# DeltaNet block on one core: a chunk's keys meet keys and queries in one product, queries meet both directions' states in one; a shorter inverse root; the last expert's down projection earlier

## The chip, the cores and the metric

The kernel runs on one core of one Trainium2 chip. The time is device microseconds of one execution, the median of three: 1802.84 us (1800.17 to 1805.5). Besides, one execution was profiled; it took 1801.21 us.

## The reference, cut to what matters

One encoder block on x of 1024 tokens by 1024 channels, in f32. One input projection of the normalised x feeds two mixers: a chunked gated linear attention (GLA, 4 heads) and a gated DeltaNet (8 heads of 128, each in both directions). After gates, a sum and an output projection comes a mixture of 32 experts, of which each token uses two, then a final RMSNorm. What one direction of a DeltaNet head computes:

```python
q, k = l2_norm(conv(q)), l2_norm(conv(k))
lower = where(strict, (k * beta) @ k.T * decay, 0)
u, w  = solve(I + lower, v * beta), solve(I + lower, k * beta * exp(g))
attn  = where(tri, q @ k.T * decay, 0)
for c in chunks:
    v_new = u[c] - w[c] @ S
    o[c]  = (q[c] * exp(g)) @ S + attn[c] @ v_new
    S     = exp(g_last) * S + k_tail[c].T @ v_new
```

## The kernel before, in words

**Number formats.** Large products (projections, experts) split each f32 operand in a high and a low fp32r part and add three products (`mm3`, L81 to L83); weights come by DMA as `wraw`, ScalarE rounds them to `whi` (L113) and VectorE takes the remainder `wlo` (L115). Small products in the DeltaNet are plain f32, and each shows as two records on TensorE (PE).

**Order.** The tile framework's scheduler puts the instructions of each engine into one order when the program is built, from the order in which the code is written and its own estimate of how long each takes. At run time each engine takes its list in that order and waits by semaphores. So a change of the code can move projection products far from the place that was edited.

**DeltaNet, 8 heads** (about 140 to 960 us of the span). Three stages per head:
- `gdn_stage1`: the projections of k, q and v, each followed by `conv` (ScalarE copies to `cin`, VectorE adds five taps at L302/L304, SiLU by ScalarE and L311) and transposes with sums of squares (L321). The keys of each 128-token chunk meet themselves (L354, tile `pgm`, four chunks of 128x128 in a bank) and the queries (L379, `pqk`). VectorE multiplies these 128x512 banks with the decays `e` into the strictly lower part M (L364) and the attention A (L382). M goes to DRAM (`xs_d`) and comes back as 32x32 blocks. VectorE inverts these in 62 instructions (`V`, L409/L411, "the solve"); the result goes to DRAM (`vs_d`, L415) and back as `Ua` (L425).
- `gdn_stage2`: per direction a transpose of `Ua` (L428), then four small groups of products that put the 32x32 inverses together (L447, L453, L461, L466, "the fix-ups"), each fed by a copy of the one before (L450, L455/L457, L463, L467). Then the scan over 8 chunks, the forward (`cf`) and the backward (`cb`) direction in turn: k·S (L479), r on VectorE (L481), q·S (L483), U·r (L486), a copy `vn` on ScalarE (L488), kt·vn (L492), the new state S on VectorE (L495), A·vn (L500). The outputs add up in `oac` (L503 to L507), and ScalarE squares them (L510).
- `gdn_stage3`: norm and gate of the outputs (inverse root L67 to L76, L529), transposes (L531), L533, and a store to `mixT`.

TensorE fills the waits of these chains with projection products (L81 to L83): those of the next heads, and 16 `gate_task`s (L276 to L280, called by `run_tasks`, two after most heads).

**After the DeltaNet** the GLA prepares its gate weights: small loads `prep` on SyncE's queue (L590, L598, L601), casts on three engines up to `ws` (L612), and its first products (L623).

**Experts.** For each expert `moe_up` (gate and up projections into `pgu`, then `sg` at L1090/L1091), `moe_down` of the expert before (`py`, `y` at L1112, and a scatter with addition by GpSimd, L1113), `moe_turn` (transposes L1097, `hh` L1100). After the last scatter the sums are read back (L1187), normalised with `rsqrt(n=2)` and stored (L1198).

**`rsqrt`** (L61): a shift, a subtraction from a magic number, a halving, then three Newton steps of three instructions.

Of the kernel before, what the change touches and what calls it, by code (L numbers as in the profile page):

```python
# [8 lines left out]
F32 = mybir.dt.float32  # L9
F32R = mybir.dt.float32r  # L10
BF = mybir.dt.bfloat16
# [7 lines left out]
P = 128  # L19
# [16 lines left out]
def hybrid_kernel(ctx: ExitStack, tc: tile.TileContext, ins, out):  # L36
# [23 lines left out]

    def rsqrt(v, n, name):  # L61

        ti = small.tile([P, n], I32, name=f"rsi{name}", bufs=1)
        y = small.tile([P, n], F32, name=f"rsy{name}")
        a = small.tile([P, n], F32, name=f"rsa{name}", bufs=1)
        xh = small.tile([P, n], F32, name=f"rsx{name}", bufs=1)
        ve.tensor_scalar(ti, v.bitcast(I32), 1, None, op0=OP.logical_shift_right)  # L67
        ve.tensor_scalar(y.bitcast(I32), ti, -1.0, RS_MAGIC, op0=OP.mult, op1=OP.add)  # L68
        ve.tensor_scalar(xh, v, -0.5, None, op0=OP.mult)  # L69
        for _ in range(3):  # L70
            if n == 1:
                ve.scalar_tensor_tensor(a, y, y, xh, op0=OP.mult, op1=OP.mult)
            else:
                ve.tensor_mul(a, y, y)  # L74
                ve.tensor_mul(a, a, xh)  # L75
            ve.scalar_tensor_tensor(y, a, 1.5, y, op0=OP.add, op1=OP.mult)  # L76
        return y

    def mm3(o, l, r, start, stop):
# [16 lines left out]
    with mix:  # L96
# [193 lines left out]
            gp.memset(zt[d], 0.0)  # L290

        def gdn_stage1(h, finish=None):
            def conv(nm, c0):
# [7 lines left out]
                a = gd.tile([P, T], F32, name="acc", bufs=5)  # L301
# [26 lines left out]

            ka = conv("k", C_DK)
# [15 lines left out]

            if finish:
                finish()
            A, M = {}, {}  # L350
            for hf in range(2):
                pgm = bank("tp", 2)
                for i in range(4):
                    te.matmul(pgm[:, i], kch[:, 4 * hf + i], kch[:, 4 * hf + i], start=True, stop=True)  # L354
                for d in range(2):
                    e = gd.tile([P, 4, P], F32, name="e", bufs=7)
                    nc.sync.dma_start(e.rearrange("p a b -> p (a b)"),
                                      dap(gcs_d, ((2 * h + d) * NT + 4 * hf) * P, [[0, P], [1, 4 * P]]))
                    with tc.issue_after(k_done):
                        ve.tensor_tensor(e, e, mneg[d][:, None, :].to_broadcast([P, 4, P]), op=OP.add)  # L360
                    for i in range(4):
                        sc.activation(e[:, i], e[:, i], AF.Exp, bias=nb[:, d, 4 * hf + i:4 * hf + i + 1])
                    m = gd.tile([P, 4, P], F32, name="m", bufs=6)
                    ve.scalar_tensor_tensor(m, pgm, -1.0, e, op0=OP.mult, op1=OP.mult)  # L364
                    for b in range(4):
                        nc.sync.dma_start(xs_d[h][d, b, 4 * hf:4 * hf + 4].rearrange("c s t -> s c t"),
                                          m[32 * b:32 * b + 32, :, 32 * b:32 * b + 32])
                    A[d, hf], M[d, hf] = e, m

            qa = conv("q", C_DQ)  # L370
            ss, _ = sumsq("q", qa)
            ve.tensor_scalar(ss, ss, 4 * EPS, None, op0=OP.add)
            rq = rsqrt(ss, NT, "q")
            rqs = small.tile([P, NT], F32, name="rqs")
            ve.tensor_scalar(rqs, rq, float(P ** -0.5), None, op0=OP.mult)
            for hf in range(2):
                pqk = bank("tp", 2)
                for i in range(4):
                    te.matmul(pqk[:, i], kch[:, 4 * hf + i],  # L379
                              qa[:, (4 * hf + i) * P:(4 * hf + i + 1) * P], start=True, stop=True)  # L380
                for d in range(2):
                    ve.tensor_tensor(A[d, hf], pqk, A[d, hf], op=OP.mult)  # L382
            va = conv("v", C_DV)
# [34 lines left out]
        def gdn_stage2(h, st):  # L418
# [52 lines left out]
            S = [None, None]  # L471
            seen = set()
            for step in range(NT):
                for d in range(2):
                    c = step if d == 0 else NT - 1 - step
                    hf, i = divmod(c, 4)
                    pc = bank("cf" if d == 0 else "cb", 1)
                    if step:
                        te.matmul(pc[:, 0], kch[:, c], S[d], start=True, stop=True)  # L479
                        r = gd.tile([P, P], F32, name=f"r{d}", bufs=1)  # L480
                        ve.scalar_tensor_tensor(r, pc[:, 0], NEG[:, d, c, h:h + 1], vtok[:, c],  # L481
                                                op0=OP.mult, op1=OP.add)
                        te.matmul(pc[:, 1], qa[:, c * P:(c + 1) * P], S[d], start=True, stop=True)  # L483
                    else:
                        r = vtok[:, c]
                    te.matmul(pc[:, 2], U[d][:, c], r, start=True, stop=True)  # L486
                    vn = gd.tile([P, P], F32, name=f"vn{d}", bufs=1)
                    sc.copy(vn, pc[:, 2])  # L488
                    if step < NT - 1:
                        kt = gd.tile([P, P], F32, name=f"kt{d}", bufs=2)  # L490
                        sc.activation(kt, ktok[:, c], AF.Copy, scale=ktl[:, d, c:c + 1])
                        te.matmul(pc[:, 0], kt, vn, start=True, stop=True)  # L492
                        Sn = gd.tile([P, P], F32, name=f"S{d}", bufs=2)
                        if step:
                            ve.scalar_tensor_tensor(Sn, S[d], DEC[:, d, c, h:h + 1], pc[:, 0],  # L495
                                                    op0=OP.mult, op1=OP.add)
                        else:
                            ve.tensor_copy(Sn, pc[:, 0])
                        S[d] = Sn
                    te.matmul(pc[:, 3], A[d, hf][:, i], vn, start=True, stop=True)  # L500
                    if step:
                        if c in seen:
                            ve.scalar_tensor_tensor(oac[:, c], pc[:, 1], EG[:, d, c, h:h + 1], oac[:, c],  # L503
                                                    op0=OP.mult, op1=OP.add)
                        else:
                            sc.activation(oac[:, c], pc[:, 1], AF.Copy, scale=EG[:, d, c, h:h + 1])
                        ve.tensor_tensor(oac[:, c], pc[:, 3], oac[:, c], op=OP.add)  # L507
                        if c in seen:
                            jk = gd.tile([P, P], BF, name="jk2", bufs=1)
                            sc.activation(jk, oac[:, c], AF.Square, accum_out=oss[:, c:c + 1])  # L510
                    else:
                        sc.copy(oac[:, c], pc[:, 3])
                    seen.add(c)
            return oac, oss, rq

# [602 lines left out]
    with tc.tile_pool(name="me", bufs=1, reuse_waits="tile") as me:  # L1118
# [22 lines left out]
        for e in range(NE + 1):  # L1141
            if e < NE:
                f = e + NX - 1
                if f < NE:
                    moe_fetch(xbs[f % NX], idx[:, f:f + 1])
                if e + 1 < NE:
                    xs[e + 1] = moe_rows(me, xbs[(e + 1) % NX])
                sg = moe_up(me, w[e], xs.pop(e))
            if e:
                moe_down(me, w.pop(e - 1), hs.pop(e - 1), idx[:, e - 1:e], roww[:, e - 1:e])  # L1150
            if e < NE:
                hs[e] = moe_turn(me, sg)
# [80 lines left out]
```

## Time and profile before

| what | value |
|---|---|
| median of 3 runs | 1802.84 us |
| profiled execution | 1801.21 us, its span 1799.4 us |
| TensorE (PE) busy | 1667.4 us, 93% |
| VectorE (DVE) busy | 1308.0 us, 73% |
| ScalarE (ACT) busy | 946.9 us, 53% |
| mean granted TensorE clock | 0.98 of full speed |

The span is what the trace covers; 1.8 us lie around it. A busy share is the sum of an engine's instructions over the span. TensorE's records overlap their successors, so its share is an upper end of what it needs.

### The profile page before, as it was taken

How to read it: one execution, taken by the hardware profiler on the slowest of the kernel's cores; microseconds unless marked ns; L12 is line 12 of the kernel's file. 1: busy time of each engine (PE TensorE's matmuls, PEld its weight loads, DVE VectorE, ACT ScalarE, POOL GpSimd, SP SyncE). 2: the span in 40 equal slices, each digit the busy share in tenths (PEclk: the TensorE clock that was granted, in tenths of full speed). 3: DMA queues.
4: the chain of work that ended last, by engine and by line, in shares of the span. 5: the costliest groups of instructions: out<-in, count | busy, mean ns of one | idle time of the engine just before them, and what ended most of it. 6: DMA issues, size and time to landing. Idle time of an engine off the chain costs nothing. (4 is left out here: it accounts for less than half of the span.)

```text
span 1799.4 us, 26981 instructions
## 1 busy us (share of the span) xinstructions
PE 1667.4 (93%) x9519; PEld 1364.1 (76%) x9519; DVE 1308.0 (73%) x2904; ACT 946.9 (53%) x2001; POOL 178.0 (10%) x184
## 2 busy tenths in 40 slices
PE   6999999999999999999999999998999799888881
PEld 5778878888888888888887888877778588666670
DVE  6787987777796877867856365565778898777773
ACT  6546464462644536445344353545355688767762
POOL 0000000000000000000001000000000243434410
PEclk9999999999999999999999999999999899999995
DMA  5322222313222232221322122214576699989965
GB/s 151 84 69 64 80 59 84 75 55 94 54 78 70 66 95 58 77 71 36 94 60 64 37 94 64 77 36 148 180 253 250 228 351 331 320 305 328 327 193 198
DMA packets 207681, 241.02 MB, mean 134 GB/s; under 512 B 72679, under 2 KB 154999, under 8 KB 207543
## 3 DMA queue, kind: packets, MB, share of 16 engines
q1 hardware_dynamic: 198327, 222.46, 38.6%
q0 software_dynamic: 9216, 16.81, 4.1%
q8 instruction: 76, 1.25, 0.3%
q14 instruction: 62, 0.51, 0.1%
HBM read 205.44 MB, written 50.53 MB: 142 GB/s over the span
## 5 line engine op out<-in xcount | busy, mean ns | idle before, releaser
L81 PE MATMUL pj<-hT_hi,whi 128*128 128x512 f32 x1168 | 470.8, 403 | 3.8 <-ACT cin L299 2.8
L83 PE MATMUL pj<-hT_hi,wlo 128*128 128x512 f32 x1168 | 470.8, 403 | 0.2 <-DVE wlo L115 0.2
L82 PE MATMUL pj<-hT_lo,whi 128*128 128x512 f32 x1168 | 470.7, 403 | 0.0
L1062 DVE TENSOR_TENSOR elo<-eraw,ehi 128x2048 fp32r<-128x2048 f32 x96 | 219.6, 2290 | 72.4 <-ACT ehi L1061 71.8
L81 PEld LDWEIGHTS pj<-hT_hi,whi 128*128 128x128 f32 x1168 | 220.9, 189 | 43.5 <-ACT cin L299 3.2
L83 PEld LDWEIGHTS pj<-hT_hi,wlo 128*128 128x128 f32 x1168 | 220.7, 189 | 37.7 <-DVE wlo L115 0.9
L82 PEld LDWEIGHTS pj<-hT_lo,whi 128*128 128x128 f32 x1168 | 220.8, 189 | 36.0
L1061 ACT CAST ehi<-eraw 128x2048 fp32r<-128x2048 f32 x96 | 184.1, 1919 | 69.9 <-DMA eraw<-in_moe_w_up_dram 56.9
L113 ACT CAST whi<-wraw 128x512 fp32r<-128x512 f32 x146 | 90.6, 621 | 160.2 <-PE pj L82 158.8
L115 DVE TENSOR_TENSOR wlo<-wraw,whi 128x512 fp32r<-128x512 f32 x146 | 100.3, 687 | 93.9 <-ACT whi L113 82.4
L304 DVE SCALAR_TENSOR_TENSOR acc<-cin,cols,acc 128x1024 f32<-128x1024 f32 x96 | 122.7, 1278 | 1.2
L81 PE MATMUL pgu<-ehi,xh 128*128 128x512 f32 x256 | 105.7, 413 | 0.0
L82 PE MATMUL pgu<-elo,xh 128*128 128x512 f32 x256 | 102.8, 402 | 0.0
L83 PE MATMUL pgu<-ehi,xl 128*128 128x512 f32 x256 | 102.4, 400 | 0.0
L1113 POOL DMA_INDIRECT acc_d<-y,idx x32 | 76.7, 2396 | 199.2 <-ACT xh L1080 74.9
L409 DVE TENSOR_TENSOR prod<-V,X 128x2 f32<-128x2 f32 (+30 forms) x248 | 85.8, 346 | 6.3
L411 DVE TENSOR_REDUCE V<-prod 128x1 f32<-128x2 f32 (+30 forms) x248 | 84.5, 341 | 5.8
L1068 POOL DMA_INDIRECT xb<-h_d,idx x32 | 66.8, 2088 | 149.3 <-ACT xb L1123 132.8
L276 ACT ACTIVATE gth<-pj 128x512 f32<-128x512 f32 x64 | 38.0, 593 | 80.0 <-PE pj L83 80.0
L83 PEld LDWEIGHTS pgu<-ehi,xl 128*128 128x128 f32 x256 | 48.9, 191 | 12.0
L81 PEld LDWEIGHTS pgu<-ehi,xh 128*128 128x128 f32 x256 | 49.3, 193 | 10.7 <-ACT xh L1080 0.2
L82 PEld LDWEIGHTS pgu<-elo,xh 128*128 128x128 f32 x256 | 49.1, 192 | 10.4
(408 smaller groups left out, 3255.1 us busy)
## 6 DMA issues: line engine op xcount, KB each, us to landing
wraw<-in_w_in_dram SPq DMA_DIRECT2D x144, 256.0 KB
eraw<-in_moe_w_gate_dram SPq DMA_DIRECT2D x64, 512.0 KB
eraw<-in_moe_w_up_dram SPq DMA_DIRECT2D x64, 512.0 KB
eraw<-in_moe_w_down_dram SPq DMA_DIRECT2D x32, 1024.0 KB
e<-gcs_d SPq DMA_DIRECT2D x32, 256.0 KB
gate_d<-gateT SPq DMA_DIRECT2D x16, 512.0 KB
xx<-in_x_dram SPq DMA_DIRECT2D x8, 512.0 KB
gin<-gate_d SPq DMA_DIRECT2D x8, 512.0 KB
```

What stands on the lines that cost most here:

```text
L81: te.matmul(o, lh, rh, start=start, stop=False)
L82: te.matmul(o, lh, rl, start=False, stop=False)
L83: te.matmul(o, ll, rh, start=False, stop=stop)
L113: sc.copy(hi, raw)
L115: ve.tensor_tensor(lo, raw, hi.bitcast(F32), op=OP.subtract)
L304: ve.scalar_tensor_tensor(a, cin[:, tp:tp + T], cw(wi, tp), a, op0=OP.mult, op1=OP.add)
L409: ve.tensor_tensor(pr_[:, :mc, :i + 1], V[:, :mc, :i + 1], X[:, i, :i + 1][:, None, :].to_broadcast([P, mc, i + 1]), op=OP.mult)
L411: ve.tensor_reduce(V[:, :mc, i], pr_[:, :mc, :i + 1], axis=AX.X, op=OP.add)
L1061: sc.copy(hi, raw)
L1062: ve.tensor_tensor(lo, raw, hi.bitcast(F32), op=OP.subtract)
L1068: gp.indirect_dma_start(out=xb, out_offset=None, in_=h2_d[:, :], in_offset=bass.IndirectOffsetOnAxis(ap=si, axis=0), bounds_check=T - 1, o ...
L1113: gp.indirect_dma_start(out=acc_d[:, :], out_offset=bass.IndirectOffsetOnAxis(ap=si, axis=0), in_=y, in_offset=None, bounds_check=T - 1, o ...
```

## The change

1. `rsqrt`: shift and subtraction become one instruction that works on the integer read as a number (times -0.5, plus the magic number); for n over 1 the halving goes too. 12 instructions become 10 (9 become 8 for n = 1).
2. `conv` writes into a tile that it is given. k and q of a head lie in one tile `kq`, so that the products k·k and k·q of a chunk are one product with 256 columns (64 instead of 128 products). A PSUM tile `pkq` holds two chunks, so VectorE takes M and A out in pieces of 128x256 instead of 128x512. All products come after q's convolution; loads and exponentials of `e` are issued before it.
3. The states of both directions stay in a tile `SK`. q·S is computed only when the scan comes to a chunk the second time, for both directions in one product of 256 columns (64 products instead of 112). The outputs of a chunk's first visit are then a plain copy.
4. For the last expert `moe_down(30)` is issued ahead of `moe_up(31)`.

```diff
-        ve.tensor_scalar(ti, v.bitcast(I32), 1, None, op0=OP.logical_shift_right)
-        ve.tensor_scalar(y.bitcast(I32), ti, -1.0, RS_MAGIC, op0=OP.mult, op1=OP.add)
-        ve.tensor_scalar(xh, v, -0.5, None, op0=OP.mult)
+        ve.tensor_scalar(y.bitcast(I32), v.bitcast(I32), -0.5, RS_MAGIC, op0=OP.mult, op1=OP.add)
...
-                ve.tensor_mul(a, a, xh)
+                ve.scalar_tensor_tensor(a, a, -0.5, v, op0=OP.mult, op1=OP.mult)
...
+            kq = gd.tile([P, 2, T], F32, name="kq", bufs=2)
+            ka, qa = kq[:, 0], kq[:, 1]
+            conv("k", C_DK, ka)
...
+                for i in (0, 2):
+                    pkq = psum.tile([P, 2, 2, P], F32, name="pkq", tag="tp", bufs=2)
+                    for j in range(2):
+                        c = 4 * hf + i + j
+                        te.matmul(pkq[:, j], kch[:, c], kq[:, :, c * P:(c + 1) * P], start=True, stop=True)
+                    for d in range(2):
+                        e = A[d, hf][:, i:i + 2]
+                        ve.scalar_tensor_tensor(M[d, hf][:, i:i + 2], pkq[:, :, 0], -1.0, e,
+                                                op0=OP.mult, op1=OP.mult)
+                        ve.tensor_tensor(e, pkq[:, :, 1], e, op=OP.mult)
...
-                        te.matmul(pc[:, 1], qa[:, c * P:(c + 1) * P], S[d], start=True, stop=True)
+                        if c in seen:
+                            ds = [o for o in range(2) if c != (0, NT - 1)[o]]
+                            te.matmul(pc[:, 2:2 + len(ds)], qa[:, c * P:(c + 1) * P],
+                                      SK[:, c, ds[0]:ds[-1] + 1], start=True, stop=True)
...
+                if e == NE - 1:
+                    moe_down(me, w.pop(e - 1), hs.pop(e - 1), idx[:, e - 1:e], roww[:, e - 1:e])
                 sg = moe_up(me, w[e], xs.pop(e))
-            if e:
+            if e and e != NE - 1:
```

The scheduler's order changes with it in most of the DeltaNet. In the changed program the line numbers of that part are about 5 higher (L447 is L452, L453 is L458, L461 is L466).

The first place is TensorE at the fix-ups of the first direction (`Ub`, `m` and `zt` are their operands; `pj` are projection products). Before, in a middle head:

```order
L447 MATMUL pz<-Ub_6924,m 32x32 x16
L82 MATMUL pj<-hT_lo,whi 128x512
L83 MATMUL pj<-hT_hi,wlo 128x512
L81 MATMUL pj<-hT_hi,whi 128x512
L82 MATMUL pj<-hT_lo,whi 128x512
L83 MATMUL pj<-hT_hi,wlo 128x512
L81 MATMUL pj<-hT_hi,whi 128x512
L82 MATMUL pj<-hT_lo,whi 128x512
L83 MATMUL pj<-hT_hi,wlo 128x512
L81 MATMUL pj<-hT_hi,whi 128x512
L453 MATMUL pu<-Ua_6918,zt_476 64x64 x8
L82 MATMUL pj<-hT_lo,whi 128x512
```

and in a middle head of the change:

```order
L81 MATMUL pj<-hT_hi,whi 128x512
L82 MATMUL pj<-hT_lo,whi 128x512
L83 MATMUL pj<-hT_hi,wlo 128x512
L452 MATMUL pz<-Ub_4443,m 32x32 x16
L458 MATMUL pu<-Ua_4437,zt_460 64x64 x8
L466 MATMUL pz<-Ub_4443,m 64x64 x8
L81 MATMUL pj<-hT_hi,whi 128x512
```

The nine projection products between the first two groups, and those before the third, now stand ahead of the first group.

The second place is TensorE at the end of the eighth head's scan (`cb` the backward direction, `mg` the transposes of the outputs). Of the change:

```order
L508 MATMUL cf<-vn_9410,e 128x128
L486 MATMUL cb<-SK,kq 128x128
L492 MATMUL cb<-SK,kq 128x128
L496 MATMUL cb<-r_9419,Ub_9142 128x128
L508 MATMUL cb<-vn_9423,e 128x128
L536 MATMUL mg<-ident,oac 128x128 x8
L81 MATMUL pj<-hT_hi,whi 128x512
```

Before, the transposes were these rows, with 27 projection products between the last product of the scan and them:

```order
L83 MATMUL pj<-hT_hi,wlo 128x512
L81 MATMUL pj<-hT_hi,whi 128x512
L82 MATMUL pj<-hT_lo,whi 128x512
L531 MATMUL mg<-ident,oac 128x128 x8
L83 MATMUL pj<-hT_hi,wlo 128x512
```

The whole scan of the eighth head has no projection product in the change, and had one to three between most steps before; behind the transposes stand 41 projection products up to the GLA's first gate product (L628), where there were 80 (up to L623).

The third place is ScalarE at the last two experts (`sg` is up, `hh` the turned hidden rows, `y` down). Before:

```order
L1100 CAST hh<-pht 128x256
L1061 CAST ehi<-eraw 128x2048
L1090 ACTIVATE sg<-pgu 128x256
L1112 ACTIVATE y<-py,roww 128x512 x2
L1100 CAST hh<-pht 128x256
```

and in the change:

```order
L1105 CAST hh<-pht 128x256
L1066 CAST ehi<-eraw 128x2048
L1117 ACTIVATE y<-py,roww 128x512 x2
L1095 ACTIVATE sg<-pgu 128x256
L1105 CAST hh<-pht 128x256
```

The rows `y` of expert 30 come ahead of `sg` of expert 31.

## Rows read from the trace of the kernel before

**Rows 1.** The page: busy time, share and instructions of each engine.
```profile
PE 1667.4 (93%) x9519; PEld 1364.1 (76%) x9519; DVE 1308.0 (73%) x2904; ACT 946.9 (53%) x2001; POOL 178.0 (10%) x184
```
**Rows 2.** Windows: a middle head; length, busy time (instructions) of each engine, clock, DMA.
```profile
480.00:590.00 110.00, 108.97 (x683) 90.46 (x681) 85.86 (x209) 52.26 (x155) 3.33 (x13) 1.00 0.27 71
```
**Rows 3.** Waits of TensorE in the DeltaNet: total us, times, longest.
```profile
PE cb L492 <- ACT vn L488: 4.6, 5, 1.0
```
**Rows 4.** Timeline, ScalarE in a scan: start us, us, what.
```profile
579.68 1.28 ACT L345 ACT_TABLE_LOAD   x1
```
**Rows 5.** Timeline, f32 products of 128 and of 256 columns (first to last record).
```profile
225.63 1.16 PE L354 MATMUL tp<-acc 128*128 128x128 f32 x8
...
1048.74 1.03 PE L740 MATMUL gpo<-gR,gqd 128*128 128x256 f32 x4
```
**Rows 6.** Groups of VectorE by form: count, busy us, mean ns, idle before.
```profile
L304 DVE SCALAR_TENSOR_TENSOR acc<-cin,cols,acc 128x1024 f32<-128x1024 f32 x93 | 118.9, 1278 | 1.0
L364 DVE SCALAR_TENSOR_TENSOR m<-tp,e 128x512 f32<-128x512 f32 x32 | 21.8, 687 | 3.9 <-ACT e L362 3.7 <-PE pz L461 0.2
...
L1091 DVE TENSOR_TENSOR sg<-pgu,sg 128x256 f32<-128x256 f32 x32 | 13.4, 418 | 2.0 <-ACT sg L1090 2.0
```
**Rows 7.** Timeline, VectorE in the last inverse roots.
```profile
1778.03 0.17 DVE L67 TENSOR_SCALAR rsif<-ssf 128x2 int32<-128x2 int32 x1
...
1778.24 0.17 DVE L68 TENSOR_SCALAR rsyf<-rsif 128x2 int32<-128x2 int32 x1
```
**Rows 8.** Timeline, three places of the tail: GpSimd's scatters of experts 29, 30, 31.
```profile
1749.45 1.55 POOL L1113 DMA_INDIRECT acc_d<-y,idx  x1 [7.23 <-ACT hh L1100]
...
1758.02 1.55 POOL L1113 DMA_INDIRECT acc_d<-y,idx  x1 [7.02 <-ACT hh L1100]
...
1765.12 1.55 POOL L1113 DMA_INDIRECT acc_d<-y,idx  x1 [5.55 <-issue]
```
**Rows 9.** Timeline, fix-ups of the eighth head, two projection products ahead of them.
```profile
903.04 0.39 PE L83 MATMUL pj<-hT_hi,wlo 128*128 128x512 f32 x1
903.27 0.39 PE L81 MATMUL pj<-hT_hi,whi 128*128 128x512 f32 x1
903.59 1.20 PE L447 MATMUL pz<-Ub,m 128*32 128x32 f32 x32
...
906.07 1.15 PE L453 MATMUL pu<-Ua,zt 128*64 128x64 f32 x16
...
908.04 1.14 PE L461 MATMUL pz<-Ub,m 64*64 64x64 f32 x16
```
**Rows 10.** Timeline, one hand-over in a scan.
```profile
946.13 0.39 PE L486 MATMUL cb<-r,Ub 128*128 128x128 f32 x2
...
946.87 0.49 PE L492 MATMUL cb<-vn,kt 128*128 128x128 f32 x2
```
**Rows 11.** Timeline, the eighth head's solve on VectorE and the transpose behind its DMAs.
```profile
863.36 0.15 DVE L409 TENSOR_TENSOR prod<-V,X 128x2 f32<-128x2 f32 x1
...
890.45 0.68 DVE L411 TENSOR_REDUCE V<-prod 128x16 f32<-128x512 f32 x1
...
901.79 1.24 DVE L428 STREAM_TRANSPOSE Ub<-Ua 128x1024 f32<-128x1024 f32 x1
```
**Rows 12.** Timeline, from the scan's last product to the GLA's first gate product.
```profile
951.82 0.49 PE L500 MATMUL cb<-vn,e 128*128 128x128 f32 x2
...
958.71 1.23 PE L531 MATMUL mg<-ident,oac 128*128 128x128 f32 x8 [0.24 <-DVE oac L529]
...
969.48 0.35 SPq L280 DMA_DIRECT2D gate_d<-gateT  x1
...
978.66 0.59 PE L623 MATMUL pz<-ws,gs 98*128 98x256 f32 x3 [0.55 <-DVE ws L612]
```
**Rows 13.** In the GLA: a wait of TensorE, and windows from its end (columns as rows 2).
```profile
1247.93 1.08 PE L679 MATMUL tp<-ident,gki 128*128 128x128 f32 x4 [4.09 <-DVE gki L675]
...
1248.00:1252.00 4.00, 4.00 (x22) 4.00 (x23) 2.71 (x8) 2.22 (x5) 0.00 (x0) 0.59 0.82 267
```

More of the change, by code (lines that the diff above doesn't have):

```diff
@@ L61, in rsqrt @@
     def rsqrt(v, n, name):
-        ti = small.tile([P, n], I32, name=f"rsi{name}", bufs=1)
         y = small.tile([P, n], F32, name=f"rsy{name}")
         a = small.tile([P, n], F32, name=f"rsa{name}", bufs=1)
-        xh = small.tile([P, n], F32, name=f"rsx{name}", bufs=1)
-        ve.tensor_scalar(ti, v.bitcast(I32), 1, None, op0=OP.logical_shift_right)
-        ve.tensor_scalar(y.bitcast(I32), ti, -1.0, RS_MAGIC, op0=OP.mult, op1=OP.add)
-        ve.tensor_scalar(xh, v, -0.5, None, op0=OP.mult)
+        ve.tensor_scalar(y.bitcast(I32), v.bitcast(I32), -0.5, RS_MAGIC, op0=OP.mult, op1=OP.add)
+        if n == 1:
+            xh = small.tile([P, n], F32, name=f"rsx{name}", bufs=1)
+            ve.tensor_scalar(xh, v, -0.5, None, op0=OP.mult)
         for _ in range(3):
@@ L72, in rsqrt @@
                 ve.scalar_tensor_tensor(a, y, y, xh, op0=OP.mult, op1=OP.mult)
+                ve.scalar_tensor_tensor(y, a, 1.5, y, op0=OP.add, op1=OP.mult)
             else:
                 ve.tensor_mul(a, y, y)
-                ve.tensor_mul(a, a, xh)
-            ve.scalar_tensor_tensor(y, a, 1.5, y, op0=OP.add, op1=OP.mult)
+                ve.scalar_tensor_tensor(a, a, -0.5, v, op0=OP.mult, op1=OP.mult)
+                ve.scalar_tensor_tensor(y, a, 1.5, y, op0=OP.add, op1=OP.mult)
         return y
@@ L292, in gdn_stage1, with conv @@
         def gdn_stage1(h, finish=None):
-            def conv(nm, c0):
+            def conv(nm, c0, a):
                 ps = proj(c0 + h * P)
@@ L300, in conv @@
                 wi = {"q": 0, "k": 8, "v": 16}[nm] + h
-                a = gd.tile([P, T], F32, name="acc", bufs=5)
                 ve.tensor_scalar(a, cin[:, 0:T], cw(wi, 0), None, op0=OP.mult)
@@ L326, in sumsq @@
                 return ss, pts
-            ka = conv("k", C_DK)
+            kq = gd.tile([P, 2, T], F32, name="kq", bufs=2)
+            ka, qa = kq[:, 0], kq[:, 1]
+            conv("k", C_DK, ka)
             k_done = conv.last.ins
@@ L350, in gdn_stage1 @@
             A, M = {}, {}
-            for hf in range(2):
-                pgm = bank("tp", 2)
-                for i in range(4):
[L354 to L370, printed above, removed]
+            for d, hf in ((0, 0), (1, 1), (1, 0), (0, 1)):
+                e = gd.tile([P, 4, P], F32, name="e", bufs=6)
+                nc.sync.dma_start(e.rearrange("p a b -> p (a b)"),
+                                  dap(gcs_d, ((2 * h + d) * NT + 4 * hf) * P, [[0, P], [1, 4 * P]]))
+                with tc.issue_after(k_done):
+                    ve.tensor_tensor(e, e, mneg[d][:, None, :].to_broadcast([P, 4, P]), op=OP.add)
+                for i in range(4):
+                    sc.activation(e[:, i], e[:, i], AF.Exp, bias=nb[:, d, 4 * hf + i:4 * hf + i + 1])
+                A[d, hf] = e
+            conv("q", C_DQ, qa)
             ss, _ = sumsq("q", qa)
@@ L376, in gdn_stage1 @@
             for hf in range(2):
[L377 to L380, printed above, removed]
                 for d in range(2):
-                    ve.tensor_tensor(A[d, hf], pqk, A[d, hf], op=OP.mult)
-            va = conv("v", C_DV)
+                    M[d, hf] = gd.tile([P, 4, P], F32, name="m", bufs=4)
+                for i in (0, 2):
[8 more added lines that the diff above has]
+                        ve.tensor_tensor(e, pkq[:, :, 1], e, op=OP.mult)
+                for d in range(2):
+                    for b in range(4):
+                        nc.sync.dma_start(xs_d[h][d, b, 4 * hf:4 * hf + 4].rearrange("c s t -> s c t"),
+                                          M[d, hf][32 * b:32 * b + 32, :, 32 * b:32 * b + 32])
+            va = gd.tile([P, T], F32, name="va", bufs=1)
+            conv("v", C_DV, va)
             vtok = gd.tile([P, NT, P], F32, name="vtok", bufs=2)
@@ L470, in gdn_stage2 @@
             oss = small.tile([P, NT], F32, name="oss")
-            S = [None, None]
+            SK = gd.tile([P, NT, 2, P], F32, name="SK", bufs=1)
             seen = set()
@@ L474, in gdn_stage2 @@
                 for d in range(2):
-                    c = step if d == 0 else NT - 1 - step
+                    c, n = (step, step + 1) if d == 0 else (NT - 1 - step, NT - 2 - step)
                     hf, i = divmod(c, 4)
@@ L478, in gdn_stage2 @@
                     if step:
-                        te.matmul(pc[:, 0], kch[:, c], S[d], start=True, stop=True)
+                        te.matmul(pc[:, 0], kch[:, c], SK[:, c, d], start=True, stop=True)
                         r = gd.tile([P, P], F32, name=f"r{d}", bufs=1)
@@ L482, in gdn_stage2 @@
                                                 op0=OP.mult, op1=OP.add)
-                        te.matmul(pc[:, 1], qa[:, c * P:(c + 1) * P], S[d], start=True, stop=True)
+                        if c in seen:
+                            ds = [o for o in range(2) if c != (0, NT - 1)[o]]
+                            te.matmul(pc[:, 2:2 + len(ds)], qa[:, c * P:(c + 1) * P],
+                                      SK[:, c, ds[0]:ds[-1] + 1], start=True, stop=True)
                     else:
                         r = vtok[:, c]
-                    te.matmul(pc[:, 2], U[d][:, c], r, start=True, stop=True)
+                    te.matmul(pc[:, 1], U[d][:, c], r, start=True, stop=True)
                     vn = gd.tile([P, P], F32, name=f"vn{d}", bufs=1)
-                    sc.copy(vn, pc[:, 2])
+                    sc.copy(vn, pc[:, 1])
                     if step < NT - 1:
@@ L492, in gdn_stage2 @@
                         te.matmul(pc[:, 0], kt, vn, start=True, stop=True)
-                        Sn = gd.tile([P, P], F32, name=f"S{d}", bufs=2)
                         if step:
-                            ve.scalar_tensor_tensor(Sn, S[d], DEC[:, d, c, h:h + 1], pc[:, 0],
+                            ve.scalar_tensor_tensor(SK[:, n, d], SK[:, c, d], DEC[:, d, c, h:h + 1], pc[:, 0],
                                                     op0=OP.mult, op1=OP.add)
                         else:
[L498 to L503, printed above, removed]
-                                                    op0=OP.mult, op1=OP.add)
[L505 to L510, printed above, removed]
+                            ve.tensor_copy(SK[:, n, d], pc[:, 0])
+                    te.matmul(pc[:, 1], A[d, hf][:, i], vn, start=True, stop=True)
+                    if c in seen:
+                        for j, o in enumerate(ds):
+                            ve.scalar_tensor_tensor(oac[:, c], pc[:, 2 + j], EG[:, o, c, h:h + 1], oac[:, c],
+                                                    op0=OP.mult, op1=OP.add)
+                        ve.tensor_tensor(oac[:, c], pc[:, 1], oac[:, c], op=OP.add)
+                        jk = gd.tile([P, P], BF, name="jk2", bufs=1)
+                        sc.activation(jk, oac[:, c], AF.Square, accum_out=oss[:, c:c + 1])
                     else:
-                        sc.copy(oac[:, c], pc[:, 3])
+                        sc.copy(oac[:, c], pc[:, 1])
                     seen.add(c)
```

## The prediction

> **What bounds the kernel now.** I read the page first, then windows over the heads, then the waits of TensorE, then timelines where the new order differs. TensorE is busy 93% of the span [rows 1], and 108.97 of 110 us in a middle head, where VectorE has 85.86 and ScalarE 52.26 [rows 2]. So in the DeltaNet the order of TensorE's list sets the time: work taken from VectorE or ScalarE is worth nothing by itself, and a place where TensorE's list holds nothing that is ready costs its whole length. The fills are projection products, one every 0.23 us [rows 9]. The other bounds are the start and the end, where single chains run. The sum below is made against the profiled 1801.21 us; the median of the runs is 1.6 us higher.
>
> **Products.** 64 pairs of k·k and k·q and 48 pairs of q·S become one product each, with the same columns. Eight records of 128 columns last 1.16 us from the first start to the last end, four of 256 columns 1.03 us [rows 5]. With the last record (0.28 and 0.38 us in such rows) taken off and the rest divided by seven and three intervals, a record costs about 0.126 and 0.217 us, so a pair of products (two records each) saves 2 x (0.252 - 0.217) = 0.07 us at most; where records follow at the closest (0.112 and 0.216) it saves 0.016. 112 pairs give 1.8 to 7.8 us. I take **-3**, nearer the close records, since that is how a full list runs.
>
> The Trainium skill, page "TensorE: Matmul & The Clock Gate", section "Back-to-back issue gap", gives about 81 ns for a 128-column product in a stream with its weight loads, and 56 by columns alone; by that difference, 25 ns for each of 224 records saved, an estimate is -5.6 in place of -3 and the sum would be 2.6 lower. By its column formula alone the saving is about half a microsecond; the rows lie between the two.
>
> **Roots.** One instruction less in the chain is worth the step from the shift to the next use, 0.21 us [rows 7]. At the end four groups run one behind the other, at the start three to four: **-0.8** and **-0.8** (bounds 0 and -1.5 each). In the heads the roots lie beside TensorE's work: 0, except behind the eighth head (below).
>
> **Last expert.** The scatters of experts 29, 30 and 31 begin at 1749.45, 1758.02 and 1765.12 [rows 8]. The last waits for the one before it to land, 7.1 us after its start; the one before waited for its rows `y` [rows 8]. With `moe_down(30)` ahead of `moe_up(31)` scatter 30 can start as soon as 29 has landed, about 1756.5, and 31 at 1763.6: **-1.5**. TensorE waits about 0.9 us for `hh` of expert 30, and that delays expert 31's rows; if these are late, the gain is 0. If everything shifts, -2.
>
> **Waits that go.** TensorE's waits in the scans are 4.6 us for `vn` of the backward direction [rows 3]; ScalarE loads activation tables, 1.28 us each, ahead of those copies [rows 4]. In the new order these loads lie outside the scans: **-5** (bounds -7 and 0).
>
> **VectorE's smaller pieces.** A 128x512 evacuation takes 0.687 us, one of 128x256 from PSUM 0.418 [rows 6]: 2 x 0.418 - 0.687 = 0.15, times eight per head, 1.2 us. VectorE has 24 us per head to spare [rows 2]: 0, unless its chain bounds the head (second rival). The first visit's plain copies on ScalarE have the same cover.
>
> **What the new order adds.**
> - Fix-ups of the first direction in six middle heads. Before, L453 starts 2.48 us after L447 and L461 1.97 after L453, with projection products between [rows 9]. Bare, the second and third group still wait for a copy of the one before. A group's own products are about 1.0 to 1.1 us [rows 9]; with the copy and two hand-overs the distance cannot be much under 1.8. So TensorE stands about 0.8 + 0.75 us: 6 x 1.5 = **+9** (bounds +4 and +11).
> - Ahead of the fix-ups TensorE has about 256 projection products, 58 us at 0.227 each, and some 5 us of transposes since the last scan. VectorE now puts three convolutions of a later head (tap 1.278 us [rows 6]) between the 62 steps of the solve, which alone took 27 us and needs 13 us more through DRAM to the transpose's end [rows 11]. I count 52 to 58 us to the solve's end, 65 to 71 with the DMAs, against 63: zero to several us per head. I take 0.5 in six heads, **+3** (bounds 0 and +30).
> - Scans. A hand-over from product to product through another engine takes 0.74 us [rows 10]. In the new order about 28 more places have only two or three products between; each lacks some 0.2 us: **+5** (bounds 0 and +10). In the eighth head the scan is bare. Its 62 products with their 256-column ones and the rest of the fix-ups are 19.4 us of work; a step needs about three hand-overs, 2.4 us, so eight steps are 19 us as well, and two directions that take turns never fit perfectly: **+3.5** (bounds +2 and +6).
> - Behind that scan. The outputs' chain takes 951.82 to 958.71 = 6.9 us from last product to transposes [rows 12]; less three foreign instructions of VectorE (0.6 each) and two steps of the root (0.4) that is 4.7, of which the product covers 0.3. No projection lies there now: **+4.4** (bounds +3 and +6).
> - From transposes to the GLA's first gate product it was 958.71 to 978.66 = 20 us [rows 12]. The store of a gate (`gate_d`) stood in SyncE's queue ahead of the last `prep` loads until 969.48 [rows 12]; in the new order it has gone before, which takes some 4.6 us off: 15.4. The cover is 1.2 us of transposes and 41 products, 9.3 us: **+4.7** (bounds 0 and +8).
>
> **Sum.** -3 - 0.8 - 0.8 - 1.5 - 5 = -11.1; 9 + 3 + 5 + 3.5 + 4.4 + 4.7 = +29.6; together +18.5. From 1801.21 that is 1819.7, and with 1.6 to the median **1821 us**. The places are unfilled not because there is less work but because it has moved to where TensorE was full already.
>
> **Rivals.** About 0.3%, 5.4 us, is what a measurement of this kernel can tell from no change.
> - *Bare places are paid already* (faster). If TensorE comes late to the fix-ups and the scans, because the products ahead of them take longer than the scheduler thought, copies and states are ready, and the fix-ups, tight scans and the wait ahead of them cost nothing. Then the gains stay, and of the end of the DeltaNet about half: -11.1 + 4.5 = **1796**. For it: TensorE waited in all scans only 4.6 us for `vn` [rows 3]. Against it: a fix-up hangs on the product just before it, so no earlier delay can help.
> - *Half of it* (the same): the bare places at their lower bounds, some +11 against -11: **1803**. The edits as such then do what they say and are worth 0.
> - *VectorE's chain bounds a head* (slower still). At 4 us in place of 0.5 ahead of the fix-ups in six heads: 21 more, **1842**. It decides once VectorE's way from scan to transpose is over 63 us.
> - *TensorE's clock falls behind the bare places.* After a wait of 4.09 us the granted clock was 0.59 on average over the next 4 us [rows 13], mostly at 1.2 in place of 2.4 GHz, about 1.6 us lost. The two waits of 4.4 and 4.7 us at the DeltaNet's end are as long. Twice 1.6 gives **1824**. The Trainium skill, page "TensorE: Matmul & The Clock Gate", section "HAM oscillation — how this bites in real kernels", says the same, that waits between bursts cost the array its full clock; by that rule these two waits are paid twice, and the trace agrees.
>
> **How the numbers follow.** Forecast 0.42, clock 0.10, VectorE's chain 0.13: slower 0.65. Half of it: same 0.18. Paid already: faster 0.17. The likeliest case alone spans 1809 to 1832. The range reaches from the faster rival to just over VectorE's chain, 1796 to 1843, which leaves out some 0.08 on either side.
>
> **What would show it.** Right: in the changed profile L458 and L466 wait for ACT or DVE copies about 0.7 us each in six heads; L536 of the eighth head waits over 4 us for L534; L628 waits over 4 us for `ws`; waits on `vn` behind table loads are gone; the last scatter starts 1 to 2 us sooner before the end than before. Wrong: L458 and L466 without a wait, a busy share of TensorE in middle heads as before (99%), or the period of a middle head (110 to 113 us) shorter. VectorE's chain would show as waits at L452 for L433 of several us.

## The result: slower by 2.8%, and the profile after

The changed kernel takes 1850.13 us (median of 4 runs, 1847.33 to 1858.59) against 1801.51 us beside it: a ratio of 1.0279, 95% interval 1.0263 to 1.0295. The forecast was slower, 1821 us; the loss is 49 us in place of 19, and lies outside the range that ended at 1843.

The page of the changed kernel:

```profile
PE 1689.8 (92%) x9295; PEld 1366.8 (74%) x9295; DVE 1292.3 (70%) x2904; ACT 949.8 (51%) x2001; POOL 174.6 (9%) x184
```

A window over a middle head of it (columns as in [rows 2]):

```profile
632.00:750.00 118.00, 114.54 (x683) 92.46 (x682) 85.81 (x220) 55.83 (x162) 3.33 (x13) 1.00 0.26 69
```

From the first product of one scan to that of the next a middle head takes 117.6 us; before, by the same mark, it was 114.3 in the later heads and 102, 95 and 108 in the first three, so the window of 110 us in [rows 2] is less than a whole head.

No engine has more to do than before. TensorE has 224 records fewer, as the merged products make it, and yet its busy time is 22.4 us longer [rows 1]. In the scan below an f32 product of 128 columns shows 0.49 us, where the next doesn't follow closely, while four in a row shared 1.16 us in [rows 5]. So part of the lost time hides in the busy time. One milestone shows where it lies: the GLA's first gate product started at 978.66 [rows 12] and now starts at 1036.66, 58.0 us later. From there to the end of the span it was 820.7 us and is now 808.8. Of these 11.9 us, 43 projection products that now stand ahead of the milestone (2825 in place of 2782) are 9.8 (0.227 each); the other 2.1 are gained somewhere behind it. So the DeltaNet and the start lost 48.2 us. TensorE's waits there, in total us, times and longest (changed kernel, 60 to 1010 us; the single row behind it is of the kernel before, 60 to 970 us):

```profile
PE tp L320 <- DVE kq L310: 11.1, 8, 3.1
PE pu L458 <- issue: 5.7, 6, 0.9
PE mg L536 <- DVE oac L534: 3.8, 7, 1.2
PE pz L466 <- DVE Ub L460: 3.6, 6, 0.7
...
PE cb L502 <- ACT vn L498: 0.4, 2, 0.2
...
PE pz L452 <- DVE Ub L433: 0.3, 1, 0.3
```

```profile
PE tp L321 <- DVE acc L311: 2.2, 2, 1.9
```

The fix-ups (L458, L466) wait 9.3 us in six heads, as forecast; for L458 the profile names no releaser ("issue"). The wait for `vn` behind table loads, 4.6 us before [rows 3], is gone. The wait at L452, where VectorE's chain would have shown, is 0.3. What the prediction didn't have is the first row, 11.1 us against 2.2: transposes of keys and queries stand in TensorE's list before VectorE has done the convolution.

The eighth head's scan and what follows, on TensorE (the first and the last product of the scan, the backward direction's U·r at some of its steps in between, one stretch of the second half in full, then the transposes and the GLA):

```profile
977.49 0.49 PE L496 MATMUL cf<-vtok,Ua 128*128 128x128 f32 x2
...
984.87 0.49 PE L496 MATMUL cb<-vtok,Ub 128*128 128x128 f32 x2 [0.36 <-DVE Ub L472]
...
988.36 0.49 PE L496 MATMUL cb<-r,Ub 128*128 128x128 f32 x2
...
991.96 0.49 PE L496 MATMUL cb<-r,Ub 128*128 128x128 f32 x2
...
999.73 0.38 PE L496 MATMUL cb<-r,Ub 128*128 128x128 f32 x2
...
1002.99 0.49 PE L508 MATMUL cf<-vn,e 128*128 128x128 f32 x2 [0.44 <-DVE SK L504]
1003.66 0.46 PE L486 MATMUL cb<-SK,kq 128*128 128x128 f32 x2 [0.19 <-DVE oac L513]
1004.57 0.70 PE L492 MATMUL cb<-SK,kq 128*128 128x256 f32 x2 [0.45 <-DVE r L488]
1005.11 0.38 PE L496 MATMUL cb<-r,Ub 128*128 128x128 f32 x2
...
1010.50 0.38 PE L496 MATMUL cb<-r,Ub 128*128 128x128 f32 x2
...
1016.26 0.49 PE L508 MATMUL cb<-vn,e 128*128 128x128 f32 x2 [0.35 <-ACT vn L498]
1021.36 1.97 PE L536 MATMUL mg<-ident,oac 128*128 128x128 f32 x8 [4.61 <-DVE oac L534]
1036.66 0.71 PE L628 MATMUL pz<-ws,gs 98*128 98x256 f32 x4 [3.19 <-DVE ws L617]
```

The bare scan, with only two projection products at its start, lasts from 977.49 to 1016.75, 39.3 us. The backward direction begins 7.4 us after the forward one, as its fix-ups lie between. A step of both directions then takes 3.5 to 4.1 us in the first half (988.36 to 991.96) and 5.0 to 5.4 us in the second (1005.11 to 1010.50), where q·S comes in. The same scan as windows (columns as in [rows 2]): before, with 70 projection products in it, then in the changed kernel, then in the run with seven tiles below, which has this scan with 72:

```profile
912.44:952.31 39.87, 39.87 (x270) 31.89 (x268) 20.10 (x57) 18.03 (x58) 1.20 (x2) 1.00 0.09 28
```

```profile
977.49:1016.75 39.26, 31.95 (x189) 23.05 (x186) 17.89 (x53) 14.83 (x52) 1.20 (x2) 1.00 0.03 7
```

```profile
933.43:973.62 40.19, 40.19 (x260) 32.22 (x258) 20.65 (x58) 17.12 (x58) 1.19 (x2) 1.00 0.08 27
```

So projections in this scan were nearly free. With 0.227 us taken off for each, the rest of the scan fits into 24.0 us where the list is full, and takes 38.8 bare. The waits of 4.61 and 3.19 us behind it are the forecast ones, the second smaller than forecast (4.4 and 4.7).

The tail, GpSimd's scatters of experts 29, 30 and 31 in the changed kernel, the last half of `y` and the first instruction of the last roots; 30 now waits for 29 to land, and 31 no longer for 30 (the second half of its own rows `y` ends at 1810.26, so I take it that it waits for these; the profile names a queue entry of ScalarE):

```profile
1795.51 1.55 POOL L1118 DMA_INDIRECT acc_d<-y,idx  x1 [5.20 <-ACT y L1117]
...
1802.42 1.55 POOL L1118 DMA_INDIRECT acc_d<-y,idx  x1 [5.37 <-DMA acc_d<-y,idx]
...
1809.57 0.69 ACT L1117 ACTIVATE y<-py,roww 128x512 f32<-128x512 f32 x1 [0.44 <-PE py L83]
...
1810.53 1.55 POOL L1118 DMA_INDIRECT acc_d<-y,idx  x1 [6.56 <-ACTq L1175]
...
1824.41 0.17 DVE L65 TENSOR_SCALAR rsyf<-ssf 128x2 int32<-128x2 int32 x1
```

Scatter 30 starts 6.9 us after 29 [rows 8: 8.6], scatter 31 8.1 after 30 [rows 8: 7.1]: 15.0 for both in place of 15.7. The last roots (first row L65) begin 21.1 us before the end of the span, where it was 21.4 [rows 7], and from scatter 29 to the end it is 50.0 us as before (49.9).

### The profile page after: what moved, and what is told of

It reads as the page before. It is cut to its first block, busy times and chain, and to the rows that moved or that the text cites. A ratio compares the mean times of both kernels' runs of the same rounds, so it can differ in the third digit from the quotient of the medians.

```text
span 1845.5 us, 26652 instructions
## 1 busy us (share of the span) xinstructions
PE 1689.8 (92%) x9295; PEld 1366.8 (74%) x9295; DVE 1292.3 (70%) x2904; ACT 949.8 (51%) x2001; POOL 174.6 (9%) x184
## 5 line engine op out<-in xcount | busy, mean ns | idle before, releaser
L303 DVE SCALAR_TENSOR_TENSOR kq<-cin,cols,kq 128x1024 f32<-128x1024 f32 x64 | 82.0, 1281 | 0.3
L1073 POOL DMA_INDIRECT xb<-h_d,idx x32 | 62.7, 1960 | 146.9 <-DVE vals L956 130.7
L501 ACT ACTIVATE kt<-ktok,ktl 128x128 f32<-128x128 f32 x112 | 44.2, 401 | 36.5 <-PE cf L502 21.4
L83 PEld LDWEIGHTS pgu<-ehi,xl 128*128 128x128 f32 x256 | 49.3, 193 | 11.9
## 6 DMA issues: line engine op xcount, KB each, us to landing
eraw<-in_moe_w_gate_dram SPq DMA_DIRECT2D x64, 512.0 KB, 17.3
```

The source lines that it names most:

```text
L83: te.matmul(o, ll, rh, start=False, stop=stop)
L1073: gp.indirect_dma_start(out=xb, out_offset=None, in_=h2_d[:, :], in_offset=bass.IndirectOffsetOnAxis(ap=si, axis=0), bounds_check=T - 1, o ...
```

## The experiments

The change alters two counts of buffers that the prediction didn't weigh: tiles `e` (decays, then the attention A) from seven to six, `m` (M) from six to four. A head needs four of each. Theory A says that this is the cause, by way of the scheduler's order. The change also gives the convolutions other buffers: five tiles for all before, now two double tiles `kq` and one `va`.

**Merged product alone, six tiles.** Edit: the change's `gdn_stage1` in the kernel before, nothing else.

> Of the change only the merged product of keys with keys and queries, with its six buffers of e and four of m; scan, roots and last expert as before. Theory A (the buffers: with six tiles e, two for the next head, half of the products wait until the scan gives tiles back, and the scheduler then moves the projections away from the fix-ups and from the last scan): nearly the whole loss is here, about 1845 us, the fix-ups' second group waiting 0.9 us in six heads and the last scan without projections. Rival B (the loss is the sum of all parts, the scan's order above all): half of it, about 1825. Rival C (the scan with both directions' states costs it): no loss here, about 1800.

Measured: 1895.54 us, ratio 1.0509 (1.0463 to 1.0555). The whole loss and 44 us more is in this part. TensorE's waits of this run (60 to 1080 us):

```profile
PE pz L452 <- DVE Ub L433: 14.7, 6, 2.5
PE tp L320 <- DVE kq L310: 9.7, 9, 2.3
PE mg L536 <- DVE oac L534: 9.6, 8, 4.9
PE pu L458 <- issue: 5.7, 6, 0.9
```

Two successive heads of it, as windows (the clock is the last figure but two):

```profile
582.60:708.00 125.40, 119.22 (x693) 97.88 (x694) 86.39 (x223) 56.66 (x163) 3.32 (x13) 0.95 0.24 66
708.00:828.20 120.20, 113.74 (x693) 93.09 (x693) 86.38 (x223) 56.65 (x163) 3.32 (x13) 1.00 0.26 69
```

The order is what theory A said: L458 waits 0.9 us in six heads, and the last scan has no projection product. Here VectorE's chain does bound each head: TensorE waits up to 2.5 us at L452. In every second of these heads the granted clock falls too (0.95), and the head is 5 us longer. All three estimates were too low.

**Merged product alone, seven tiles.** Edit, against the run before:

```diff
-                e = gd.tile([P, 4, P], F32, name="e", bufs=6)
+                e = gd.tile([P, 4, P], F32, name="e", bufs=7)
```

> As the run before, but seven tiles e in place of six (four of m as there), nothing else. Theory A: the order is that of before in shape, projections between the fix-ups and in the last scan, and the time is 1797 to 1808. If the merged product, its late place after the queries' convolution or VectorE's smaller pieces cost the time themselves, it is as slow as the run with six, about 1840.

Measured: 1821.60 us, 1.0093 (1.0072 to 1.0114). One tile is worth 74 us here, with nothing else changed, and projections are back between fix-ups and in the last scan. But 18 us stay, and neither estimate was right. The first waits are now

```profile
PE tp L320 <- DVE kq L310: 14.1, 7, 3.7
PE tp L394 <- ACT vtok L395: 2.6, 6, 0.5
```

and the one for L452 is not among them.

**Scan alone.** Edit: the change's scan in the kernel before, with six tiles `e` and four `m` for its room.

> Of the change only the scan: both directions' states in one tile, queries at the second visit alone; with six tiles e and four m, since the tile takes their room. Keys' and queries' products, roots and last expert as before. Theory A: within 6 us of before, 1797 to 1808. Rival C (the scan costs it): 1825 to 1850.

Measured: 1806.64 us, 1.0019 (1.0010 to 1.0029). The scan costs 3 us and rival C falls. The smaller counts do little harm with the old stage, at most these 3 us: it is their meeting with the merged product.

**The whole change with seven tiles.** Edit (and `bufs=7` as above):

```diff
-            SK = gd.tile([P, NT, 2, P], F32, name="SK", bufs=1)
+            SK = gd.tile([P, NT - 2, 2, P], F32, name="SK", bufs=1)
+            sl = lambda c: {0: 3, NT - 1: NT // 2}.get(c, c) - 1
...
-                        te.matmul(pc[:, 0], kch[:, c], SK[:, c, d], start=True, stop=True)
+                        te.matmul(pc[:, 0], kch[:, c], SK[:, sl(c), d], start=True, stop=True)
```

> The whole change, but with seven tiles e; the room comes from the states' tile, which has six places in place of eight (chunks 0 and 7 use those of 3 and 4 after their second visit). Theory A: the whole loss goes, 1792 to 1806, and the gains of the shorter roots and the last expert (2 to 3 us) show. Rivals B and C: at least 1820.

Measured: 1822.07 us, 1.0109 (1.0087 to 1.0131): 28 us better than the changed kernel, by one tile `e` and the smaller state tile that makes room for it. Theory A's time is missed. The eighth head has its fill again, its GLA wait is 0.3 us (L629 there). The merged products show the tile: the two halves of one head's products begin 66.0 us apart in the changed kernel (483.83 and 549.85, the second in the scan of the head before), and some 8 us apart here (498.6 and 506.7). The solve shows what the order did. First and last instruction of one solve on VectorE, changed kernel, then this run:

```profile
571.62 0.16 DVE L414 TENSOR_TENSOR prod<-V,X 128x2 f32<-128x2 f32 x1
...
621.73 0.68 DVE L416 TENSOR_REDUCE V<-prod 128x16 f32<-128x512 f32 x1
```

```profile
532.90 0.16 DVE L414 TENSOR_TENSOR prod<-V,X 128x2 f32<-128x2 f32 x1
...
559.99 0.68 DVE L416 TENSOR_REDUCE V<-prod 128x16 f32<-128x512 f32 x1
```

50.8 us in place of 27.8, because three convolutions of a later head lie between its steps. (So in six heads of the changed kernel; this run has 27.8 in its last four heads, 33 to 46 in the first four.) The way from the scan's last product to the fix-ups is then 65.4 us (568.80 to 634.15) against 56.5 before (503.86 to 560.38). The list fills it with 256 projection products, where it had 237, and from scan to scan it has 336 in each of the first six intervals, where the first three had 261, 260 and 311: so the gate projections were used up before the eighth head. Why the scheduler turns one tile into this order was not tried. 19 us stay here too: TensorE waits for transposes of keys and queries and of values,

```profile
PE tp L320 <- DVE kq L310: 11.7, 4, 4.3
PE tp L394 <- DVE va L310: 5.6, 3, 2.9
```

of which one on the timeline is

```profile
525.16 0.33 PE L394 MATMUL tp<-ident,va 128*128 128x128 f32 x1 [2.90 <-DVE va L310]
```

The two rows are 17.3 us together; L321, the like of L320 before, waited 2.2.

**Eight tiles.** Edit: `bufs=8` in the run with the merged product alone.

> Of the change only the merged product of keys with keys and queries, now with eight tiles e (four for the next head) and four of m; the scan is that of before. If the tiles are the whole matter (theory A), the 18 us that seven tiles left go as well: 1797 to 1808. If the rest comes from the late place of the products behind the queries' convolution, or from twice as many evacuations of half the size that now all fall in the scan (theory D: VectorE is full there, and the next head's convolutions and the transposes behind them come late), it stays at 1812 to 1825.

Measured: 1820.25 us, 1.0099 (1.0081 to 1.0117). No gain over seven, so the rest isn't a matter of tiles `e`. All these runs have four tiles `m` and the new buffers of the convolutions; whether these have a part in the rest was not tried.

**Late, but apart, seven tiles.** Edit, against the merged product with seven:

```diff
-                for i in (0, 2):
-                    pkq = psum.tile([P, 2, 2, P], F32, name="pkq", tag="tp", bufs=2)
...
+                pgm, pqk = bank("tp", 2), bank("tp", 2)
+                for i in range(4):
+                    c = 4 * hf + i
+                    te.matmul(pgm[:, i], kch[:, c], kch[:, c], start=True, stop=True)
...
+                for d in range(2):
+                    ve.scalar_tensor_tensor(M[d, hf], pgm, -1.0, A[d, hf], op0=OP.mult, op1=OP.mult)
```

> As the run with seven tiles e and the merged product alone, in the same late place, but the products are apart again (128 of 128 columns) and VectorE takes M and A out in pieces of 128x512: half as many evacuations, 1.2 us less per head. If the halved evacuations cost the rest (theory D): 1800 to 1810, and TensorE's waits for transposes of keys and queries (L320) fall from 14 us to under 6. If the late place alone costs it: 1815 to 1825.

Measured: 1809.69 us, 1.0040 (1.0025 to 1.0055). Of the 18 us, 11 go when the evacuations are whole again, though the products are apart. The other 7 stay with the late place and with what the run keeps besides, the four tiles `m` and the convolutions' buffers; it doesn't separate these. The wait for L320 fell from 14.1 less than expected, which accounts for half of the 11, to

```profile
PE tp L320 <- DVE kq L310: 8.6, 5, 4.0
```

**All but the merged product.**

> The whole change without the merged product of keys with keys and queries (its stage as before, with six tiles e and four m). The scan alone cost 3.3 us, roots and last expert should give 2 to 4: 1798 to 1806, so the merged product and its tiles are the whole loss. If the parts work on each other: over 1810.

Measured: 1807.15 us, 1.0024 (1.0014 to 1.0033). The loss is the merged stage, as said. But the time is 1 us above what was expected, 4.7 above the kernel before, where the scan alone (+3.3) and roots and last expert alone (-2.9, next run) add up to 0.4. So these parts don't simply add; what costs the other 4 was not looked for.

**Roots and last expert alone.**

> Of the change only the shorter inverse root and the last expert's order. By the sum of the prediction -0.8 at the start, -0.8 at the end, -1.5 at the last expert: 1798 to 1801, at most 0.3% faster. If roots move the order of the heads too: up to 6 us either way.

Measured: 1800.15 us, 0.9984 (0.9974 to 0.9994): 2.9 us by the ratio, 3.1 by the prediction's sum. This version beats both kernels, if by little. The places are not those of the sum, though. The three scatters take 15.2 us (1748.44 to 1763.65) in place of 15.7, the last roots are 0.3 shorter, and 2.3 us are gained ahead of the GLA's first gate product, which starts at 976.41.

**Fill held for the eighth head.** Two edits of the changed kernel; the first:

```diff
+        held = {h: [tasks.pop() for _ in range(n)] for h, n in ((GDN_H - 1, 1), (GDN_H - 2, 0))}
...
-                    te.matmul(pu[:, c], z[half(rb), c], u[half(rb), c, half(rb)], start=True, stop=True)
+                    gdn_stage2.fx = te.matmul(pu[:, c], z[half(rb), c], u[half(rb), c, half(rb)], start=True, stop=True).ins
...
             run_tasks(2 if h else 1)
+            with tc.issue_after(gdn_stage2.fx):
+                for t in held.get(h, ()):
+                    gate_task(*t)
```

> The changed kernel, but the last gate projection is queued on TensorE behind the eighth head's last fix-up, so that this head's scan and the stretch behind it have projections again (64 and 21 rows, none before); ahead of its fix-ups 63 are left of 191. If the bare scan and the two waits behind it are lost time for want of the fill at that place (theory E), the time falls by about 20 us, to 1830. If the fill is only short (theory F: the stretch from the seventh scan through the solve and the DMAs to the fix-ups lasts 45 us whatever TensorE does in it), the loss moves there, a wait of about 25 us at the first fix-up, and the time stays at 1845 to 1855.

Measured: 1865.29 us, 1.0327 (1.0293 to 1.0361). The wait at the eighth head's first fix-up, and a window from the last 6.7 us of it on, with a clock of 0.50:

```profile
PE pz L452 <- DVE Ub L433: 23.4, 2, 23.2
```

```profile
960.00:985.00 25.00, 15.48 (x145) 13.70 (x146) 6.37 (x11) 2.95 (x8) 0.13 (x1) 0.50 0.20 43
```

Theory F holds in the main: of the 29 us of projections taken away there (128 products), 23.2 came back as a wait. The stretch became 5.7 us shorter all the same, so it doesn't last 45 us whatever TensorE does. The time is higher than F said. The clock stood at half for 27 us behind that wait (966.66 to 993.5), with TensorE busy for 24 of them, so up to 12 us are lost by an estimate; that this is the whole difference is not shown. The filled scan takes 45.7 us here, at a mean clock of 0.83.

The second holds one task there and two behind the seventh head's fix-up (the two counts are 1 and 2).

> The changed kernel with one gate projection queued behind the eighth head's last fix-up and two more behind the seventh's: fill for the eighth head comes out of the sixth and seventh (208 rows ahead of the seventh's fix-ups in place of 256, 127 ahead of the eighth's in place of 191). If a middle head is bound by TensorE's work (its list is full and the chain through VectorE has room), those heads shorten by what is taken away and the time falls by about 20 us, to 1830. If a middle head is bound by its chain from scan to fix-ups (65 us), they don't shorten: waits of 10 us at each of the two first fix-ups, and 1840 to 1850.

Measured: 1868.21 us, 1.0336 (1.0296 to 1.0377). In the seventh and eighth head (780 to 1000 us):

```profile
PE pz L452 <- DVE Ub L433: 19.0, 2, 11.9
```

Of the two estimates neither holds alone. In the seventh head 48 projection products, 10.9 us, were taken away ahead of the fix-ups; 7.1 us of them came back as a wait, and the way from scan to fix-ups fell from 65.4 to 61.6 us. So VectorE's chain lies only some 4 us below TensorE's full list there, and as long as the list is full it is the list that sets the head's length. In the eighth head 64 fewer products (14.5 us) left a wait of 11.9. Both runs miss their time on the high side; behind the two waits of this one the clock was at half too, 26 us each time (869.1 to 895 and 971.7 to 997.5).

## Why the prediction was wrong

**Right.** *Fix-ups*: +9 forecast, 9.3 measured. *Behind the scan*: +4.4 and +4.7 forecast, 4.61 and 3.19 measured. *Waits that go*: -5, and 4.2 of the 4.6 us went. *Roots and last expert*: -3.1 forecast, -2.9 when made alone, but by luck: in that run the last roots gave 0.3 where 0.8 was forecast, the scatters 0.5 where it was 1.5, and most of the gain lies ahead of the GLA.

**Wrong.** The step that failed most in its size is *Scans*, "eight steps are 19 us as well, and two directions that take turns never fit perfectly: +3.5". It makes the bare scan 22.9 us; it lasts 39.3. I took three hand-overs a step (2.4 us; at 0.74 each it is 2.2), as if the two directions ran beside each other from the start. They don't: the backward one begins 7.4 us late, and a step is 3.5 to 4.1 us, then 5.0 to 5.4. In the second half the list puts one direction's U·r behind the other's A·vn, and A·vn waits 0.44 us behind the state (L504 in the rows above). Against the old scan, with the projections of both taken off, the bare one lost 14.8 us (38.8 less 24.0) where 3.5 were forecast. The old scan's 39.9 us had the same length, but under a full list, so this row alone could not have told it.

The second failure is a term that was put at nothing. "VectorE has 24 us per head to spare: 0, unless its chain bounds the head" costed the smaller evacuations so. The transposes behind late convolutions wait: L320 11.1 us in the changed kernel against 2.2. With seven tiles the runs put 11 us on the halved evacuations, in product and evacuation together, and 7 on the late place and what came with it. That the evacuations' bunch in the scan delays the convolutions is argued; half of the 11 us shows as shorter waits for L320. The term for VectorE's chain, +3, didn't come: 0.3 at L452.

Third, the clock was a rival of its own with 0.10, priced at 3 us. It belonged to the forecast. In the changed kernel it fell at the eighth head's end, and in the second head's fix-ups too, where no long wait stands:

```profile
282.00:286.00 4.00, 4.00 (x29) 3.04 (x29) 1.18 (x4) 0.30 (x1) 0.00 (x0) 0.50 0.51 148
286.00:290.00 4.00, 4.00 (x36) 3.38 (x35) 1.42 (x4) 0.73 (x3) 0.00 (x0) 0.50 0.00 0
1016.00:1021.00 5.00, 0.49 (x2) 0.30 (x2) 3.20 (x16) 1.59 (x5) 0.00 (x0) 0.72 0.00 0
1021.00:1026.00 5.00, 4.64 (x17) 4.08 (x18) 3.45 (x15) 0.00 (x0) 0.00 (x0) 0.60 0.21 84
```

Eight us at half are up to 4 us lost in the second head alone, by an estimate: TensorE was busy throughout.

Where the time went, by stretches of the two traces: us of each stretch with 0.227 taken off for each projection product in it, and the sum of the forecast's terms for the same stretch.

| stretch | before | change | lost | forecast |
|---|---|---|---|---|
| to the first scan (151.99, now 167.93) | 52.6 | 57.8 | 5.3 | -0.8 |
| seven heads, first scan to eighth | 268.5 | 288.1 | 19.6 | 9 |
| eighth scan | 24.0 | 38.8 | 14.8 | 3.5 |
| from there to the GLA's first gate product | 2.1 | 10.6 | 8.5 | 9.1 |
| behind it | | | -2.1 | -2.3 |

This adds up to 46.1 us, the difference of the two profiled spans; the medians differ by 48.6. The forecast's 18.5 lacks 11.3 in the bare scan, 10.6 in the seven heads, where the waits for L320 and the clock belong, and 6.1 at the start, which nothing here explains in full. What is shown is the cause of the order: one tile `e` takes 74 us off the merged product alone, and with the smaller state tile 28 off the changed kernel. The prediction names these counts nowhere; it took the new order from the schedule, and priced the places in it.

*Rivals.* Paid already and half of it fell: a fix-up does hang on the product before it. The lower bounds that make up the rival of the same time add to 9, not 11. VectorE's chain was right of the merged product alone, in its place (L452, 14.7 us) and as what sets a head's length; in the changed kernel the list covered it, by some 4 us in the seventh head. *Products* (-3) can't be told from this; it is lost in waits either way.

## What to carry to other kernels

When a change trims a pool to make room, ask of each count how many tiles the next iteration can have while this one holds its own, and look at the scheduler's order with the count put back: here one tile of 2 KB per partition was worth more than all the products saved. A stretch whose engine is always busy can hide a chain that is nearly as long: the eighth scan kept its 39 us when 70 products left it, and a middle head gave back 3.8 of 10.9 us. Price a merged operation by its evacuations as well as by the products it saves.

## What was not expected of the hardware

The clock fell to half in places without a long wait. In the second head TensorE had waits of only 0.95 and 0.58 us at the fix-ups, yet the granted clock was 0.50 from 282 to 290 us; in four like heads after it, it stayed at 1.00. In the run with the merged product and six tiles every second of the middle heads shows it (0.95 against 1.00) with the same list, and is 5 us longer. The Trainium skill, page "TensorE: Matmul & The Clock Gate", section "HAM oscillation — how this bites in real kernels", describes a clock that falls when the wait for a DMA between two bursts of matmuls is long, so that the next burst starts slow. The eighth head's 4.61 us ahead of its transposes agree with that (0.60 behind them); the second head's 0.95 and 0.58 us are no such waits. What ended the full clock there is open: small products (32x32 and 64x64 tiles) and the two short waits went before it. That the same list falls in one head and not in the next is what these rows add.
